# Attention gate's weights split ahead of the third pair's rows, and two steps between a late weight's maximum and its use

## The chip, the cores and the metric

The kernel runs on one core of one Trainium2 chip. The metric is the device time of one execution in microseconds (us). A core has TensorE (PE in the profile, with its weight loads as PEld), VectorE (DVE), ScalarE (ACT), GpSimd (POOL) and SyncE (SP), which issues most of the DMAs. Each engine works through its own list of instructions in order and waits on semaphores for the others.

## The reference, cut to what matters

A one-layer encoder block is applied to two batches of 2048 tokens by 1024 features. Cut to its core:

```python
u = _rmsnorm(h, g_norm)
z = u @ w_in                      # 1024 x 2304
q, k, v, ga, f, gf = jnp.split(z, cuts, axis=-1)   # 512, 128, 128, 512, 512, 512
q = rope(_rmsnorm(q, g_q)); k = rope(_rmsnorm(k, g_k))
a = _blocked_gqa(q, k, v) * jax.nn.silu(ga)        # 8 heads, 2 kv heads, width 64
fo = _fourier_branch(f, w_fmix) * jax.nn.silu(gf)
h = h + jnp.concatenate([a, fo], axis=-1) @ w_out
gate = jax.nn.sigmoid(_rmsnorm(h, g_ple) @ w_ple_gate)
h = h + (p @ w_ple) * gate
y = _rmsnorm(h, g_final)
```

All inputs are float32.

## The kernel before, in words

A float32 product is made of three float16 products. Each operand is split into a high and a low half: ScalarE writes the high half (a scaled copy), VectorE the low half (scaled value minus high half), and TensorE multiplies high by high, high by low and low by high. For a weight the scale is a power of two from the maximum of the whole matrix. So a weight is handled in three stages: eight loads of 128 rows each; eight `tensor_reduce` of VectorE to w_mx (L312), their maximum per partition (L320) and a maximum over partitions by GpSimd (`partition_all_reduce`, p_mm, L322); then VectorE's few instructions on one column that make the scale (`pow2_all`, L269 to L280, whose first writes p_p at L272), and eight splits, each one instruction of ScalarE (L334) and one of VectorE (L335).

The kernel has two phases. In the projection phase, which fills something over a quarter of the span, `project` (L560) handles the tokens in chunks of two tiles of 128 rows ("pairs"). For a chunk it loads the rows x, squares them on ScalarE (`sq_u`), makes the row norm by Newton steps on VectorE (`newton`, result rsq_z at L258), splits the normed rows (`hi_u` on ScalarE at L634, `lo_u` on VectorE at L643, tile hl), and lets SP issue DMA transposes from hl to uc (L438). TensorE then multiplies uc with the q and kv weights (`mm_tile`), and a "sweep" (`sweep_chunk`, L897) multiplies it with f, gf and ga (the attention gate). A sweep gives ScalarE a scaled copy ft or a tanh th (L921, L954) and a copy ge (L913), and VectorE a gt or gat (L956) with its maximum tmax (L944). GpSimd issues the stores of gt, ge and gat. Behind it come the attention and the rest, into which the late parts are filled.

PSUM has eight banks, which `bank` (L169) hands out in a fixed rotation: five ps_x, one ps_f and two ps_g. A bank can be written again only after its readers are done.

The order of instructions on all engines is written out by hand: `manual_schedule` keeps every engine's instructions in the order in which the Python code emits them. Python generators make the order: `next(g)` lets a generator emit its next step, and `until(g, "split")` runs it until it has emitted the last split of a weight.

Ahead of the loop over chunks, L831 to L895 of `project` write the start by hand. The generators there are wkv and wq (kv and q weights) and bg, which goes through f, gf, ga and then the six late weights (`weight_far`, L341: w_out, w_ple_gate and w_ple, each in two halves of 512 columns), the rows p and the channel map. Before the change the lines from L875 run: split gf; a part of the first sweep; square, norm and split the rows of the third pair (number 2: `sq_u(2)`, `newton`, `hi_u(2)`, `lo_u` with its two transposes), three loads of x, and then the whole handling of ga up to its last split (L883), the first w_out loads, a further part of the sweep, and the tables of `mid()`.

A late weight is loaded twice, once for its maximum and once for the split, whose result is stored to DRAM. `weight_far` emits a load per step, the `tensor_reduce` of each (L357), then `scale` (L362): the maximum per partition (L368), the maximum over partitions (in `pow2`, L266), and the scale, all in one step. Three steps later come the splits (L384, L387). In the projection phase a step of bg is taken once in five steps of the sweep (`NBF`, in `sweep_part`), and `defer` emits at once, so a step's place among the sweep's instructions is fixed by that count.

On GpSimd a row named ISA stands ahead of each `partition_all_reduce` of a late weight, and another ahead of the tensor operations that follow it.

Of the kernel before, what the change touches and what calls it, by code (L numbers as in the profile page):

```python
# [10 lines left out]
F32 = mybir.dt.float32  # L11
# [13 lines left out]
W_EXP = 14  # L25
# [115 lines left out]
class Build:  # L141
# [199 lines left out]
    def weight_far(self, name, src, cols, g, pool):  # L341

        nc, st = self.nc, self.st
        sl, ahead, nk = {}, AH, src.shape[0] // 128

        def load(j):
            if j < 2 * nk:
                sl[j] = pool.tile([128, 512], F32, name="w_st", tag="w2k", bufs=self.nw2k)
                nc.sync.dma_start(sl[j][:, :cols], src[j % nk * 128:(j % nk + 1) * 128, :])

        for j in range(ahead):
            load(j)
            yield
        mx = st.tile([128, 8], F32, name="w_mx")
        for k in range(nk):
            load(k + ahead)
            self.defer(lambda w=sl.pop(k), k=k: nc.vector.tensor_reduce(  # L357
                out=mx[:, k:k + 1], in_=w[:, :cols], op=ALU.max, axis=AX.X, apply_absolute_value=True))
            yield
        f = [None] * nk  # L360

        def scale():  # L362
            m = mx
            if g is not None:
                m = st.tile([128, 8], F32, name="w_m2")
                nc.vector.tensor_tensor(out=m[:], in0=mx[:], in1=g[:], op=ALU.mult)
            m1 = st.tile([128, 1], F32, name="w_m1")
            nc.vector.tensor_reduce(out=m1[:], in_=m[:, :nk], op=ALU.max, axis=AX.X, apply_absolute_value=True)  # L368
            s, self.sc[name] = self.pow2("w_" + name, m1[:], W_EXP)
            f[:] = [s[:]] * nk  # L370
            if g is not None:
                gs = st.tile([128, 8], F32, name="w_gs")
                nc.vector.tensor_scalar(out=gs[:], in0=g[:], scalar1=s[:], scalar2=None, op0=ALU.mult)
                f[:] = [gs[:, k:k + 1] for k in range(nk)]

        self.defer(scale)
        self.wd[name] = nc.dram_tensor("wd_" + name, (128, 2, nk, cols), F16, kind="Internal").ap()
        for _ in range(3):
            yield
        for k in range(nk):  # L380
            load(k + nk + ahead)
            w = sl.pop(k + nk)
            o = pool.tile([128, 2, 512], F16, name="w_o", tag="w2k", bufs=self.nw2k)
            nc.scalar.activation(o[:, 0, :cols], w[:, :cols], AF.Copy, scale=f[k])  # L384

            def low(k=k, w=w, o=o):
                nc.vector.scalar_tensor_tensor(out=o[:, 1, :cols], in0=w[:, :cols], scalar=f[k], in1=o[:, 0, :cols],  # L387
                                               op0=ALU.mult, op1=ALU.subtract)
                nc.sync.dma_start(self.wd[name][:, :, k, :], o[:, :, :cols])

            self.defer(low)
            yield
# [167 lines left out]
    def project(self, P, PU, W, early, wkv, wq, wga, bg, mid):  # L560
# [3 lines left out]
        nc, st = self.nc, self.st  # L564
# [27 lines left out]
        def sq_u(i):  # L592
            SU[i] = st.tile([128, CH], F32, name="n_su", bufs=3)
            for tt in range(CH):
                j = P.tile([128, 2 * DM], F16, name="jk", tag="sq", bufs=1)
                nc.scalar.activation(j[:, :DM], X[i][tt][:], AF.Square, accum_out=SU[i][:, tt:tt + 1])
# [6 lines left out]
        def newton(iq, iu, sq):  # L603
            ms = P.tile([128, 11 * CH], F32, name="n_ms", bufs=2)
            q, u = ms[:, :10 * CH].rearrange("p (t h) -> p t h", t=CH), ms[:, 10 * CH:]
            if sq is not None:
                ss = P.tile([128, CH, 10], F32, name="q_ss", bufs=2)
                nc.vector.tensor_reduce(out=ss[:], in_=sq[:], op=ALU.add, axis=AX.X)
                for m, sl, _, _ in heads:
                    nc.vector.tensor_scalar(out=q[:, :, sl], in0=ss[:, :, sl], scalar1=self.sc["ms_" + m][:],  # L610
                                            scalar2=EPS, op0=ALU.mult, op1=ALU.add)
            else:
                nc.vector.memset(ms[:, :10 * CH], 1.0)
            if iu is not None:
                nc.vector.tensor_scalar(out=u, in0=SU.pop(iu)[:], scalar1=1.0 / DM / U_SC ** 2,
                                        scalar2=EPS / U_SC ** 2, op0=ALU.mult, op1=ALU.add)
            else:
                nc.vector.memset(u, 1.0)
            r = self.rsqrt(ms[:], 11 * CH, "q", st=P)
            if iu is not None:  # L620
                R[iu] = r[:, 10 * CH:]
            if sq is not None:
                rq = r[:, :10 * CH].rearrange("p (t h) -> p t h", t=CH)
                rs = P.tile([128, CH, 10], F32, name="q_rs", bufs=2)
                for m, sl, _, _ in heads:
                    nc.vector.tensor_scalar(out=rs[:, :, sl], in0=rq[:, :, sl], scalar1=self.sc["inv_" + m][:],
                                            scalar2=None, op0=ALU.mult)
                return rs

        def hi_u(i):  # L630
            HL[i] = []
            for tt in range(CH):
                hl = PU.tile([128, 2, DM], F16, name="hl", bufs=2)
                nc.scalar.activation(hl[:, 0, :], X[i][tt][:], AF.Copy, scale=R[i][:, tt:tt + 1])  # L634
                HL[i].append(hl)
# [110 lines left out]
        def sweep_part(us):  # L746

            while us > 0 and sweeps:
                try:
                    us -= next(sweeps[0])  # L750
                    if done:
                        done.append(True)
                        if len(done) % NBF == 0:
                            next(bg, None)
                        if len(done) % NBF == 2:
                            next(self.ahead, None)
                except StopIteration:
                    del sweeps[0]
# [16 lines left out]
        def until(g, word):  # L775
            while next(g) != word:
                pass
# [97 lines left out]
        until(bg, "split")  # L875
        sweep_part(10.4)
        sq_u(2)
        newton(None, 2, None)
        hi_u(2)
        both(lo_u, 2)  # L880
        load_x(3, 1)
        both(load_x, 4)
        until(bg, "split")  # L883
        next(bg)
        done.append(True)
        sweep_part(11.6)
        mid()
# [967 lines left out]
```

## Time and profile before

| what | value |
|---|---|
| median of 3 runs | 2743.02 us (2740.77 to 2745.37) |
| profiled execution | 2747.83 us |
| its span | 2746.0 us |
| granted TensorE clock, mean | 0.991 |
| busy: PE, DVE, ACT, POOL | 96%, 62%, 44%, 59% |
| TensorE's wait for the ga split | 7.34 us, ended at 91.20 us |
| TensorE's next long wait | 6.15 us, ended at 144.13 us |
| VectorE's waits for the maximum over partitions of the six late weights | 39.1 us in 6 waits |

A row of the timeline gives the start (us from the span's start), how long the merged instructions took, the engine, the line, the operation with its tiles and the count; the brackets at its end say how long the engine was idle ahead of it and which instruction ended that. SPq is SyncE's queue of issued DMAs. A row of the waits gives who waited for whom: total, times, longest. A row of the DMA view gives the median time from issue to landing.

### The profile page before, as it was taken

Reading aid. Unit: us, or ns where it says so; the run is one execution under the profiler, and the core shown is the slowest. Engines: PE = TensorE matmul, PEld = TensorE weight load, DVE = VectorE, ACT = ScalarE, POOL = GpSimd, SP = SyncE. Lnnn points to the kernel's source line nnn. Section 1 sums busy time; section 2 is a strip of 40 time slices with the busy share of each in tenths; the row PEclk is TensorE's granted clock in tenths of the full one; section 3 lists DMA queues with packets and bytes.
Section 4 is the critical chain, followed back from the end, with each engine's and each line's share of the span. In section 5 each row is a group of like instructions: output and inputs, shape, how many; then the busy total and the mean of one; then the engine's idle time right before and its main releaser. Section 6 shows DMA issues by size and latency. Waiting matters only on the chain.

```text
span 2746.0 us, 46196 instructions
## 1 busy us (share of the span) xinstructions
PE 2649.2 (96%) x18176; PEld 1261.7 (46%) x18176; DVE 1702.8 (62%) x2477; ACT 1213.0 (44%) x2047; POOL 1631.3 (59%) x1394
## 2 busy tenths in 40 slices
PE   6899999999998998999999999999999999999998
PEld 3455565655555553444434444344444334444443
DVE  6755555564455775666666666666666667666644
ACT  3434333342224553454544555445545445444442
POOL 1223323242335886777777777777777777777760
PEclk9999999999999999999999999999999999999999
DMA  7567567675427662122222223322222222222223
GB/s 233 144 177 199 163 192 189 180 189 118 140 71 229 215 215 83 45 60 63 74 61 60 55 67 81 88 63 69 56 79 58 64 70 68 58 72 74 58 68 76
DMA packets 418554, 296.73 MB, mean 108 GB/s; under 512 B 259456, under 2 KB 360000, under 8 KB 418336
## 3 DMA queue, kind: packets, MB, share of 16 engines
q1 hardware_dynamic: 405424, 252.01, 35.0%
q0 software_dynamic: 12912, 41.77, 4.2%
q8 instruction: 142, 2.33, 0.4%
q14 instruction: 76, 0.62, 0.1%
HBM read 149.50 MB, written 86.51 MB: 86 GB/s over the span
## 4 chain that ended last, share of the span: by engine, by line
PE 86%; DVE 6%; issue 2%; DMA 2%; ACT 1%; POOL 1%; SPq 0%; DVEq 0%; ACTq 0%; POOLq 0%
PE ps_g L1473 22%; PE ps_o L1205 16%; PE ps_x L445 15%; PE ps_s L1141 13%; PE ps_f L445 6%; PE ps_g L445 6%; PE ps_m L1168 4%; PE ps_f L1237 1%; DVE a_mx L1176 1%; PE ps_f L1191 1%; PE ps_g L1012 1%; PE ps_g L1060 1%; DVE w_mx L312 1%; ACT p L1144 0%; PE ps_x L911 0%
## 5 line engine op out<-in xcount | busy, mean ns | idle before, releaser
L1149 POOL TENSOR_TENSOR acc<-acc,p 128x1024 f32<-128x1024 f32 x384 | 910.7, 2372 | 217.8 <-ACT p L1144 172.7
L1176 DVE TENSOR_REDUCE a_mx<-ps_m 128x1 f32<-128x1024 f32 x499 | 610.1, 1223 | 529.9 <-PE ps_m L1168 520.8
L1144 ACT ACTIVATE p<-ps_s,s_scale 128x512 f32<-128x512 f32 x1024 | 647.2, 683 | 659.1 <-PE ps_s L1141 645.6
L1473 PE MATMUL ps_g<-w_pg,hT 64*128 64x512 f16 x2784 | 494.8, 377 | 5.8 <-DMA hT<-h_hl 5.7
L1205 PE MATMUL ps_o<-p,v 128*64 128x512 f32 x2048 | 466.1, 597 | 0.0
L445 PEld LDWEIGHTS <-uc 128*128 128x128 f16 x3072 | 301.3, 98 | 311.8 <-issue 22.4
L1141 PE MATMUL ps_s<-q,k 64*128 64x512 f16 x3072 | 435.0, 378 | 4.9 <-ACT p L1144 4.8
L1473 PEld LDWEIGHTS <-hT 64*128 64x128 f16 x2784 | 200.2, 94 | 165.3 <-issue 20.7
L1141 PEld LDWEIGHTS <-k 64*128 64x128 f16 x3072 | 149.6, 94 | 250.8 <-issue 128.0
L1473 PE MATMUL ps_g<-w_wo,mh 64*128 64x512 f16 x1440 | 261.6, 378 | 1.4 <-DVE seen L1439 1.4
L1205 PEld LDWEIGHTS ps_o<-p,v 128*64 128x64 f32 x2048 | 141.7, 137 | 257.3 <-issue 248.2
L1473 PE MATMUL ps_g<-w_wo,mT 64*128 64x512 f16 x1440 | 256.7, 377 | 0.6 <-DMA mT<-mh 0.6
L1168 PE MATMUL ps_m<-k,q 64*128 64x512 f16 x998 | 202.3, 377 | 11.4 <-DVE a_mx L1176 9.6
L1147 POOL TENSOR_TENSOR acc<-p,p 128x1024 f32<-128x1024 f32 x64 | 150.7, 2354 | 97.7 <-ACT p L1144 97.0
L445 PEld LDWEIGHTS <-w_ga 128*128 128x128 f16 x1536 | 151.4, 99 | 53.7 <-issue 23.3
L928 POOL DMA_DIRECT2D gfd<-gt x32 | 19.2, 601 | 216.0 <-DVE gt L956 211.1
L1473 PEld LDWEIGHTS <-mh 64*128 64x128 f16 x1440 | 99.3, 94 | 89.6 <-issue 14.5
L1473 PEld LDWEIGHTS <-mT 64*128 64x128 f16 x1440 | 100.6, 94 | 84.6 <-issue 2.3
L1221 ACT ACTIVATE tb<-ps_o,a_scale 64x256 f32<-64x256 f32 x128 | 60.0, 469 | 167.4 <-PE ps_o L1205 166.6
L445 PE MATMUL ps_x<-uc,w_ga 128*128 128x256 f16 x1008 | 115.8, 276 | 6.8 <-ACT ge L913 6.2
L1244 DVE RECIPROCAL ps_f<-ps_f 128x256 f32<-128x256 f32 x61 | 107.1, 1756 | 14.2 <-PE ps_f L1237 14.2
L946 POOL DMA_DIRECT2D agd<-gat x64 | 35.8, 559 | 134.7 <-DVE gat L956 134.5
(331 smaller groups left out, 3404.2 us busy)
## 6 DMA issues: line engine op xcount, KB each, us to landing
q<-qTd SPq DMA_DIRECT2D x256, 64.0 KB, 2.2
ag<-agd SPq DMA_DIRECT2D x64, 256.0 KB, 3.3
out<-h POOLq DMA_DIRECT2D x31, 512.0 KB, 3.0
x<-in_x_prompt SPq DMA_DIRECT2D x16, 512.0 KB, 5.6
w_st<-in_w_out SPq DMA_DIRECT2D x32, 256.0 KB, 4.3
gfd<-gt POOLq DMA_DIRECT2D x32, 256.0 KB, 3.2
gd<-ge POOLq DMA_DIRECT2D x32, 256.0 KB, 3.6
agd<-gat POOLq DMA_DIRECT2D x64, 128.0 KB, 2.4
```

The costliest lines, as they stand in the source:

```text
L445: self.nc.tensor.matmul(ps, lhs(ia, k), rhs(ib, k), start=(i == 0), stop=(i == 3 * ks - 1))
L946: nc.gpsimd.dma_start(self.agd[s][1, r * 128:(r + 1) * 128, c * n:(c + 1) * n], gt[:, :n])
L1141: nc.tensor.matmul(S[u][e][:], w[sl], q[sl].rearrange("p h q -> p (h q)"), start=j == i == 0, stop=i + 1 == len(todo), skip_group_check=True)
L1144: nc.scalar.activation(p[:, e, :], S[u][e][:], AF.Exp, scale=self.sc["s_scale"][:])
L1147: nc.gpsimd.tensor_tensor(out=ACC[u][:], in0=P[u, 0][:], in1=p[:], op=ALU.add)
L1149: nc.gpsimd.tensor_tensor(out=ACC[u][:], in0=ACC[u][:], in1=p[:], op=ALU.add)
L1168: nc.tensor.matmul(ps[c], Q[u][0][sl, h, :], kt[s, kv, half][sl, :, 0, :], start=True, stop=True)
L1176: nc.vector.reduce_max(MX[u][:, h, half, c:c + 1], x, axis=AX.X)
L1205: nc.tensor.matmul(o[64 * e:64 * e + 64, :], vt[s, kv, c // 8][:, c % 8, :], p[:, e, :], start=(j == 0), stop=(j == 7))
L1221: nc.scalar.activation(tb[64 * e:64 * e + 64], ov[64 - 64 * e:128 - 64 * e, e], AF.Copy, scale=self.sc["a_scale"][64 - 64 * e:128 - 64 * e ...
L1244: nc.vector.reciprocal(r, r)
L1473: nc.tensor.matmul(g[0][:], g[1](ia, k)[sl], g[2](ib, k)[sl], start=a, stop=z, skip_group_check=True)
```

## The change

In `project` the ga weight's eight maxima and its maximum over partitions (nine steps of bg) are emitted right behind `sq_u(2)`, and its scale and its eight splits right behind the third pair's norm. The split of the third pair's rows (`hi_u(2)`, `lo_u`, the transposes) and the three loads of x follow. Before, ga came behind all of these. The first w_out loads come behind the x loads, before and after.

In `weight_far` the maximum over partitions stays in `scale`, but the instructions that use it (`pow2_all` and the column scales) are a function of their own, `factors`, which is emitted two steps later; the splits follow one step behind it, three behind `scale` as before.

```diff
@@ weight_far
         f = [None] * nk
+        mm = st.tile([128, 1], F32, name="p2_mm")
 
         def scale():
...
             nc.vector.tensor_reduce(out=m1[:], in_=m[:, :nk], op=ALU.max, axis=AX.X, apply_absolute_value=True)
-            s, self.sc[name] = self.pow2("w_" + name, m1[:], W_EXP)
+            nc.gpsimd.partition_all_reduce(mm[:], m1[:], 128, bass_isa.ReduceOp.max)
+
+        def factors():
+            s, self.sc[name] = self.pow2_all("w_" + name, mm, W_EXP)
             f[:] = [s[:]] * nk
...
         self.defer(scale)
...
-        for _ in range(3):
+        for _ in range(2):
             yield
+        self.defer(factors)
+        yield
@@ project
         sq_u(2)
+        for _ in range(9):
+            next(bg)
         newton(None, 2, None)
+        until(bg, "split")
+        next(bg)
         hi_u(2)
         both(lo_u, 2)
         load_x(3, 1)
         both(load_x, 4)
-        until(bg, "split")
-        next(bg)
         done.append(True)
```

On TensorE and on SP the order of instructions is the same before and after the change; on GpSimd too, but for buffer numbers. On ScalarE the two high halves of the third pair move behind the eight splits of ga. VectorE's order changes there and at five of the six late weights. The lines of the changed kernel are 1 to 8 higher than the same lines before.

## The prediction

> **What bounds the kernel now.** I read the page first (busy times, chain), then what TensorE waited for, then the timelines of all queues from 70 to 300 us, where the change lies.
>
> ```profile
> span 2746.0 us, 46196 instructions
> PE 2649.2 (96%) x18176; PEld 1261.7 (46%) x18176; DVE 1702.8 (62%) x2477; ACT 1213.0 (44%) x2047; POOL 1631.3 (59%) x1394
> PE 86%; DVE 6%; issue 2%; DMA 2%; ACT 1%; POOL 1%; SPq 0%; DVEq 0%; ACTq 0%; POOLq 0%
> ```
>
> TensorE (PE) is busy 96% of the span and is 86% of the chain that ended last. Nothing behind the projection rests on a clock time, so what TensorE's stream loses or wins early is carried to the end. What counts is therefore TensorE's waits up to 300 us, by what it waited for (total, times, longest):
>
> ```profile
> PE ps_f L445 <- ACT w_ga L334: 7.3, 1, 7.3
> PE ps_x L445 <- ACT ge L913: 6.2, 1, 6.2
> PE ps_g L445 <- DVE gat L956: 5.5, 3, 3.4
> ```
>
> The first is the wait for the attention gate's split (w_ga), the second ends at 144 us, the longest of the third at 296 us. TensorE's timeline at these places and between them:
>
> ```profile
> 91.20 0.61 PE L445 MATMUL ps_f<-uc,w_ga 128*128 128x256 f16 x2 [7.34 <-ACT w_ga L334]
> 104.60 5.34 PE L445 MATMUL ps_x<-wr_q,uc 128*128 128x512 f16 x24
> 122.76 5.34 PE L445 MATMUL ps_f<-w_gf,uc 128*128 128x512 f16 x24
> 128.19 1.12 PE L911 MATMUL ps_x<-ft,dft 128*128 128x512 f32 x2
> 144.13 5.28 PE L445 MATMUL ps_x<-uc,w_ga 128*128 128x256 f16 x24 [6.15 <-ACT ge L913]
> 295.79 4.45 PE L445 MATMUL ps_g<-uc,w_ga 128*128 128x256 f16 x24 [3.44 <-DVE gat L956]
> ```
>
> **Part 1: the gate's split goes ahead of the third pair's rows.** On VectorE (DVE), between the end of the gf weights' split and the gate's scale, before the change (rsq_z is the third pair's row norm, hl its low half, w_mx the gate's maxima, p_p the first step of its scale):
>
> ```order
> L258 TENSOR_TENSOR rsq_z_738<-rsq_z_733,rsq_w 128x22
> L643 SCALAR_TENSOR_TENSOR hl<-x,rsq_z_738,hl 128x1024 x2
> L312 TENSOR_REDUCE w_mx<-w_qn 128x1 x2
> L312 TENSOR_REDUCE w_mx<-w_t_418 128x1 x2
> L312 TENSOR_REDUCE w_mx<-w_t_589 128x1 x2
> L312 TENSOR_REDUCE w_mx<-w_t_592 128x1 x2
> L317 TENSOR_TENSOR w_m_768<-w_mx,gn 128x8
> L320 TENSOR_REDUCE w_m_770<-w_m_768 128x1
> L272 TENSOR_SCALAR p_p<-p_mm 128x1
> ```
>
> and where hl stands now, behind the last of the gate's splits:
>
> ```order
> L335 SCALAR_TENSOR_TENSOR w_ga<-w_t_592,w_gs,w_ga 128x512 x2
> L284 TENSOR_SCALAR inv_ga<-w_ga_i 128x1
> L284 TENSOR_SCALAR h_ga<-inv_ga 128x1
> L649 SCALAR_TENSOR_TENSOR hl<-x,rsq_z_753,hl 128x1024 x2
> L964 SCALAR_TENSOR_TENSOR gt<-th,ps_x 128x512
> L357 TENSOR_REDUCE w_mx<-w_st 128x1
> L964 SCALAR_TENSOR_TENSOR gt<-th,ps_g 128x512
> ```
>
> The maxima now start right behind h_gf, the norm fills the wait for POOL, and the two hl stand just ahead of the first L357. That one reduces the first rows of w_out, so it waits for their load. On SyncE's queue (SP) nothing is reordered; this piece is the same in both:
>
> ```order
> L438 DMA_TRANSPOSE uc<-hl 128x16x128 x2
> L589 DMA x<-in_x_prompt 128x1024 x3
> L349 DMA w_st<-in_w_out 128x512 x3
> ```
>
> So the transposes of hl, which now come late, hold back three x loads and the w_out loads. The rows for the sum:
>
> ```profile
> 75.48 0.15 DVE L284 TENSOR_SCALAR h_gf<-inv_gf 128x1 f32<-128x1 f32 x1
> 77.65 0.17 DVE L615 TENSOR_SCALAR n_ms<-n_su 128x2 f32<-128x2 f32 x1 [1.99 <-ACT jk L596]
> 81.42 2.48 DVE L643 SCALAR_TENSOR_TENSOR hl<-x,rsq_z,hl 128x1024 f16<-128x1024 f32 x2 [1.22 <-ACT hl L634]
> 83.81 1.27 DVE L312 TENSOR_REDUCE w_mx<-w_qn 128x1 f32<-128x512 f32 x2
> 88.88 0.16 DVE L320 TENSOR_REDUCE w_m<-w_m 128x1 f32<-128x8 f32 x1
> 89.59 0.15 DVE L272 TENSOR_SCALAR p_p<-p_mm 128x1 f32<-128x1 f32 x1 [0.55 <-POOL p_mm L322]
> 96.67 0.15 DVE L284 TENSOR_SCALAR h_ga<-inv_ga 128x1 f32<-128x1 f32 x1
> 97.33 0.68 DVE L357 TENSOR_REDUCE w_mx<-w_st 128x1 f32<-128x512 f32 x1
> 80.23 2.19 ACT L634 ACTIVATE hl<-x,rsq_z 128x1024 f16<-128x1024 f32 x2 [2.61 <-DVE rsq_z L258]
> 90.42 1.33 ACT L334 ACTIVATE w_ga<-w_qn,w_gs 128x512 f16<-128x512 f32 x2 [8.01 <-DVE w_gs L328]
> 82.73 4.52 SPq L438 DMA_TRANSPOSE uc<-hl  x2
> 87.31 1.81 SPq L589 DMA_DIRECT2D x<-in_x_prompt  x3
> 89.16 1.84 SPq L349 DMA_DIRECT2D w_st<-in_w_out  x3
> uc<-hl SPq DMA_TRANSPOSE x1, 4.4
> w_st<-in_w_out SPq DMA_DIRECT2D x1, 256.0 KB, 6.1
> ```
>
> The last two rows are landing times from the queue view: the first transpose, issued at 82.73, and the first w_out load, issued at 89.16.
>
> Step by step, in us of the span. After h_gf (75.63) come maxima and their maximum, 83.9 to 89.04, 5.15; the norm, 77.65 to 80.23, 2.6 with its memset; then scale and start of the split, 89.59 to 90.42, 0.8. ScalarE's first split starts at 75.63 + 5.15 + 2.6 + 0.8 = 84.2 in place of 90.42, and TensorE takes it up at 85.0 in place of 91.20: **6.2 earlier**. POOL's 0.55 is hidden by the norm; without that cover it would cost 0.55 again.
>
> The eight splits keep their pace, so h_ga ends at 96.82 - 6.2 = 90.6. There hl starts, 9.2 later than 81.42 (its high half is ready: ScalarE's splits end 6.2 earlier too, near 89.1, and one high half takes 1.1). The transposes, the x loads and the first w_out load leave SP 9.2 later: 89.16 + 9.2 = 98.4, landing 6.1 later at 104.5. VectorE is at L357 by 90.6 + 2.5 (hl) + 0.6 (gt) = 93.7, waits 10.8, and reduces at 104.5 in place of 97.33: **7.2 later**. The transposes themselves are no loss: the first is issued at 91.9 and lands 4.4 later at 96.3, ahead of TensorE, which needs it at 104.60 - 6.2 = 98.4. On ScalarE the two high halves (2.19) now stand ahead of gf's th and ge, which come 4 earlier all the same; POOL's order is unchanged. Queued behind VectorE's wait are the second gt, the g_q and g_k tables, the next row norm and the gat of the first chunk.
>
> Does TensorE feel it? It arrives 6.2 early, until it needs what VectorE and ScalarE give back:
>
> ```profile
> 116.63 0.41 DVE L956 SCALAR_TENSOR_TENSOR gat<-th,ps_f 128x256 f32<-128x256 f32 x1
> 124.71 0.69 DVE L357 TENSOR_REDUCE w_mx<-w_st 128x1 f32<-128x512 f32 x1 [7.22 <-DMA w_st<-in_w_out]
> 127.45 1.26 ACT L921 ACTIVATE ft<-ps_g,inv_f 128x512 f32<-128x512 f32 x2
> ```
>
> Bank ps_f, written at 91.20, is written next at 122.76, after the gat at 116.63 has read it. TensorE would now come at 116.6, the gat ends at 117.0 + 7.2 = 124.2: a wait of 7.6. Then the first L911 needs ft, 127.45 + 7.2; before, TensorE used it 0.7 after its start, so there was no slack, and L911 starts 7.2 late. VectorE's 7.22 wait at 124.71 moves along, since its load stands behind the next transposes on SP, which follow VectorE's next hl. The 6.15 wait at 144.13 ends behind the same chain. So TensorE passes 144.13 at 151.3: part 1 costs **+7.2**. Bounds: the load's landing. x loads and stores beside it could stretch it by one store, 3.6; 0 is the nearest case (the loads at 119 to 121 had stores beside them and landed in 6.0). The lower bound is the load landing in time, -3.6 (rival 1). I take 0.
>
> ```profile
> w_st<-in_w_out SPq DMA_DIRECT2D x3, 256.0 KB, 6.0
> gfd<-gt POOLq DMA_DIRECT2D x1, 256.0 KB, 3.6
> ```
>
> A rule against this reading: the Trainium skill, Perfetto Trace Analysis, section Optimization Strategy, says to find the gaps of the engine one optimizes for and to make what they wait for start sooner. By it, part 1 is worth -6.2, the gap that shrinks; the trace agrees that the gap is there (7.34) but has VectorE's wait at its other end.
>
> **Part 2: two steps between the maximum over partitions and its use.** It concerns the six late weights (w_out, w_ple_gate, w_ple, two halves each). The waits at the second and third:
>
> ```profile
> 203.89 0.15 DVE L272 TENSOR_SCALAR p_p<-p_mm 128x1 f32<-128x1 f32 x1 [6.88 <-POOL p_mm L266]
> 204.59 0.41 DVE L956 SCALAR_TENSOR_TENSOR gat<-th,ps_x 128x256 f32<-128x256 f32 x1
> 205.38 0.41 DVE L956 SCALAR_TENSOR_TENSOR gat<-th,ps_x 128x256 f32<-128x256 f32 x1
> 256.43 0.15 DVE L272 TENSOR_SCALAR p_p<-p_mm 128x1 f32<-128x1 f32 x1 [6.93 <-POOL p_mm L266]
> ```
>
> On VectorE at the second weight, now:
>
> ```order
> L369 TENSOR_REDUCE w_m_1945<-w_m_1943 128x1
> L964 SCALAR_TENSOR_TENSOR gat<-th,ps_x 128x256
> L952 TENSOR_REDUCE tmax_87<-gat 128x1
> L272 TENSOR_SCALAR p_p<-p_mm 128x1
> L273 TENSOR_SCALAR p_p<-p_p 128x1
> ```
>
> One gat and its tmax, which stood behind the wait, now stand inside it. At the first weight no row of VectorE lies between, so its wait (part of the chain to 144.13) stays. VectorE still waits for POOL, but has one pair, 205.38 - 204.59 = 0.79, less to do behind it. The chain of waits runs from these two places to 295.79, so the 3.44 there shrinks by up to 2 x 0.79: **-1.6**. Bounds: 0, if another releaser comes last, and -3.4, if that wait goes. At the fourth weight the scale now stands behind the next row norm; TensorE did not wait there, and the splits' stores followed that norm before too: nothing.
>
> **Sum.** +7.2 - 1.6 = +5.6. The profiled execution took 2747.83 (span 2746.0 and 1.8 around it), so 2753.4; it lies 4.8 above the median of the three runs, 2743.02, so the forecast there is **2748.6**, +0.20%. About 0.2%, 5.5 us, is what a measurement can tell from no change; the forecast lies right on that edge.
>
> **Rivals.**
> 1. *Faster: the w_out load does not hold VectorE.* Place: L357 on VectorE. Then VectorE is at 93.7 in place of 97.33, 3.6 ahead, and TensorE's second wait ends 3.6 earlier: -3.6 - 1.6 = -5.2, 2737.8. It decides at a landing before 97.33 + 1.6 = 98.9; 104.5 speaks against it, and so does SP's unchanged order. For it: nothing on SP but position holds the load. It is where the Trainium skill's rule on gaps leads. 0.14.
> 2. *No change that can be measured: +7.2, but the 3.44 wait goes entirely*: +3.8, 2746.8. For it: several steps of that chain are VectorE's, and each may win a little. Against: only 1.6 is found in the order. 0.18.
> 3. *More: the moved loads meet stores, landing 3.6 later, and part 2 gives nothing*: +10.8, 2753.8. Against: loads with stores beside them landed in 6.0. 0.08.
>
> That part 2 does not do what it says holds for the first weight, and is in the sum.
>
> **How the numbers follow.** The forecast's case has 0.60: +4 to +7.5, about 0.42 of it above 5.5 and 0.18 below. Slower 0.42 + 0.08 = 0.50; within 0.2% 0.18 + 0.18 = 0.36; faster 0.14. The range leaves out most of rival 1 and keeps rival 3: 2740.5 to 2754.
>
> **What would show it.** Right: the w_ga wait of TensorE falls from 7.3 to near 1.3; VectorE waits about 11 at the first L357 for w_st; TensorE has a new wait of some 7 at ps_f for gat and passes the stretch of 144.13 about 7 later; the wait at 295.79 (then near 303) is about 1.9. Wrong: L357 without a wait, or w_ga passed early and 144.13 passed before 144. Then rival 1 holds.

## The result, and the profile after

| kernel | median | range |
|---|---|---|
| before, 6 runs beside it | 2745.01 us | 2740.77 to 2747.75 |
| after, 6 runs | 2754.85 us | 2751.39 to 2755.97 |

The change makes the kernel slower: ratio 1.0035, 95% interval 1.0025 to 1.0046, so +9.6 us (6.9 to 12.6). The forecast was +5.6, and its range, up to 2754, ended just below the median. Before's own median was 2743.02 in the three runs that the forecast started from and 2745.01 here, so of the 6.3 us between 2748.6 and 2754.85 2.0 are the starting point and 4.3 the change. Of all executions here and in the experiments three ran far slower (3084, 4593 and 10609 us), and the ratios leave them out.

The profiled execution of after took 2751.89, near the fast end of its range, and that of before 2747.83, above its median. The pair shown here therefore differs by 4.1 us only; a second profiled execution of after, further down, took 2757.74.

The page of after, in the rows that answer to those of before:

```profile
span 2750.1 us, 46195 instructions
PE 2648.5 (96%) x18176; PEld 1260.3 (46%) x18176; DVE 1699.7 (62%) x2477; ACT 1212.9 (44%) x2047; POOL 1631.6 (59%) x1394
```

TensorE does the same work. Its waits between 80 and 320 us that come to over 0.5 us (total, times, longest):

```profile
PE ps_f L451 <- DVE gat L964: 7.4, 1, 7.4
PE ps_x L919 <- ACT ft L929: 4.6, 1, 4.6
PE ps_x L451 <- ACT ge L921: 2.9, 1, 2.9
PE ps_g L451 <- DVE gat L964: 2.9, 1, 2.9
PE ps_f L451 <- DVE w_ga L335: 1.4, 7, 0.4
PE ps_f L451 <- ACT w_ga L334: 0.9, 1, 0.9
```

The gate's wait is gone, 0.9 in place of 7.3, with seven short ones for single splits behind it (1.4 in all, in place of 0.3). Two stand here that before did not have, 7.4 at bank ps_f and 4.6 at ft. TensorE's timeline:

```profile
85.72 0.39 PE L451 MATMUL ps_f<-uc,w_ga 128*128 128x256 f16 x2 [0.91 <-ACT w_ga L334]
124.89 7.91 PE L451 MATMUL ps_f<-w_gf,uc 128*128 128x512 f16 x24 [7.44 <-DVE gat L964]
137.40 2.08 PE L919 MATMUL ps_x<-ft,dft 128*128 128x512 f32 x2 [4.59 <-ACT ft L929]
151.56 2.78 PE L451 MATMUL ps_x<-uc,w_ga 128*128 128x256 f16 x24 [2.92 <-ACT ge L921]
300.17 4.45 PE L451 MATMUL ps_g<-uc,w_ga 128*128 128x256 f16 x24 [2.90 <-DVE gat L964]
```

In this profile TensorE began its 48 matmuls of w_f, which lie ahead of everything that the change moves, at 62.22 and not at 61.27 as in before; so 0.95 comes off every later start when the two are compared. TensorE is then 6.4 early at 85.72 (forecast 6.2) and 6.5 late at 151.56, where before it passed at 144.13. VectorE, ScalarE, SP and POOL between:

```profile
91.26 2.47 DVE L649 SCALAR_TENSOR_TENSOR hl<-x,rsq_z,hl 128x1024 f16<-128x1024 f32 x2
107.30 0.69 DVE L357 TENSOR_REDUCE w_mx<-w_st 128x1 f32<-128x512 f32 x1 [12.97 <-DMA w_st<-in_w_out]
118.51 4.81 DVE L649 SCALAR_TENSOR_TENSOR hl<-x,rsq_z,hl 128x1024 f16<-128x1024 f32 x2 [0.31 <-ACT hl L640]
132.09 0.69 DVE L357 TENSOR_REDUCE w_mx<-w_st 128x1 f32<-128x512 f32 x1 [6.79 <-DMA w_st<-in_w_out]
...
103.91 1.06 ACT L602 ACTIVATE jk<-x 128x1024 f16<-128x1024 f32 x1 [8.73 <-DMA x<-in_x_prompt]
...
92.56 7.06 SPq L444 DMA_TRANSPOSE uc<-hl  x2
99.68 1.51 SPq L595 DMA_DIRECT2D x<-in_x_prompt  x3
101.24 1.90 SPq L349 DMA_DIRECT2D w_st<-in_w_out  x3
...
94.63 0.74 POOL L936 DMA_DIRECT2D gfd<-gt  x1 [12.38 <-DVE gt L964]
118.93 3.31 POOL L691 TENSOR_TENSOR qn<-z,q_rs 128x1280 f32<-128x1280 f32 x1
```

VectorE waits 13.0 us for w_out's first rows, where the forecast had a wait of 10.8, and reduces them 9.0 later than before (107.30 - 0.95 - 97.33). Two things were not forecast. The two transposes hold SP for 7.06 us in place of 4.52; two of POOL's four stores of the first sweep, which before came ten us after the transposes, now leave in the midst of them. And ScalarE waits 8.7 us too, for an x load that stands behind the same transposes. The first of these stores in the kernel before:

```profile
97.72 0.74 POOL L928 DMA_DIRECT2D gfd<-gt  x1 [8.16 <-DVE gt L956]
```

### The profile page after: what moved, and what is told of

Read it like the earlier page. It is cut to its first block, busy times and chain, and to the rows that moved or that the text cites. A ratio compares the mean times of both kernels' runs of the same rounds, so it can differ in the third digit from the quotient of the medians.

```text
span 2750.1 us, 46195 instructions
## 1 busy us (share of the span) xinstructions
PE 2648.5 (96%) x18176; PEld 1260.3 (46%) x18176; DVE 1699.7 (62%) x2477; ACT 1212.9 (44%) x2047; POOL 1631.6 (59%) x1394
## 4 chain that ended last, share of the span: by engine, by line
PE 86%; DVE 7%; DMA 3%; issue 2%; ACT 1%; POOL 1%; SPq 1%; DVEq 0%; ACTq 0%; POOLq 0%
PE ps_g L1481 22%; PE ps_o L1213 16%; PE ps_x L451 15%; PE ps_s L1149 13%; PE ps_f L451 6%; PE ps_g L451 6%; PE ps_m L1176 4%; PE ps_f L1245 1%; DVE a_mx L1184 1%; PE ps_f L1199 1%; PE ps_g L1020 1%; PE ps_g L1068 1%; DVE w_mx L312 1%; ACT p L1152 0%; PE ps_x L919 0%
```

## The experiments

The theories that the expectations speak of: *A*, the first w_out load stands behind the late transposes, VectorE waits for it, and that is the loss. *B*, part 2 costs what the forecast did not see. *C*, the third pair's rows come too late themselves, and the load is a bystander. *D*, formed after the fourth run: two transfers stand behind the transposes, and either alone holds the chain. All ratios are to the kernel before in the same job (medians 2745.8 to 2746.8 us). Lines in the experiments' kernels stand up to 14 higher; L358 and L364 are the change's L357 in the rows of w_mx.

**1. Part 1 alone.** The edit in `project` only; `weight_far` as before.

> Part 1 alone: the gate's split ahead of the third pair's rows, the late weights as before the change. Theory A (the first w_out load stands behind the late transposes on SP, VectorE waits for it, and every long wait of TensorE is followed by slow matmuls): part 1 carries the whole loss, +9 to +11 us against the kernel before, about the change's 9.7 plus the 0.5 that part 2 won at the 3.44 wait. Theory B (the loss above the forecast comes from part 2): part 1 gives the forecast's +7.2 or less, and the rest is missing here. Theory C (the third pair's rows themselves come too late, not the load): the same as A here.

Ratio 1.0034 (1.0022 to 1.0046), 2755.16 us: +9.3. Part 1 carries the whole loss, and B is out.

**2. Part 2 alone.** The edit in `weight_far` only.

> Part 2 alone: the two steps between a late weight's maximum over partitions and its use, the start as before the change. Theory A: between -1.6 and 0 us, most likely -0.5, what the traces show at the wait near 296. Theory B: slower by 2 to 5 us, from instructions that the scale now stands behind at the later weights. Theory C says nothing on it.

Ratio 1.0000 (0.9991 to 1.0009), 2745.41 us. The waits for the maximum over partitions do get shorter, 25.1 us in all in place of 39.1, and TensorE's wait behind them hardly does:

```profile
DVE p_p L272 <- POOL p_mm L370: 25.1, 5, 6.8
```

and in TensorE's timeline:

```profile
296.06 4.43 PE L451 MATMUL ps_g<-uc,w_ga 128*128 128x256 f16 x24 [2.75 <-DVE gat L962]
```

2.75 in place of 3.44: 0.7 us, and the matmuls behind it are as slow as before (4.43 for 24). The interval, 2.5 us to either side, can't tell -0.7 from the forecast's -1.6; the row can.

**3. The change with w_out's first two loads ahead of the third pair's transposes.** No other engine's order changes.

```diff
@@ weight_far
+        pre = 2 if name == "wo0" else 0
+        for j in range(pre):
+            load(j)
+        if pre:
+            yield
         for j in range(ahead):
-            load(j)
+            if j >= pre:
+                load(j)
             yield
...
-            load(k + ahead)
+            if k + ahead >= pre:
+                load(k + ahead)
@@ project
         until(bg, "split")
         next(bg)
+        next(bg)
         hi_u(2)
```

> The changed kernel with w_out's first two loads issued on SP ahead of the third pair's transposes; nothing else changes its place. Theory A: the first L357 has no wait, VectorE is there near 94.4 in place of 107.3, three ahead of before; the wait at the fourth L357 stays, since its load is still behind the next transposes, but ends some 3 earlier than in the kernel before; total -3 to -5 us against before, -12 to -14 against the change. Theory C: the first L357's wait goes, but TensorE still waits at ps_f or ft for VectorE or ScalarE work behind the late rows, and the total stays 3 us or more above before.

Ratio 1.0016 (1.0007 to 1.0024), 2750.28 us: +4.4, half the loss, not the gain that A asked for. The first L357 has no wait now (93.31). VectorE, then ScalarE, then TensorE:

```profile
107.39 1.49 DVE L621 TENSOR_REDUCE q_ss<-sq 128x20 f32<-128x1280 f32 x1 [8.36 <-ACT sq L613]
...
104.91 1.06 ACT L609 ACTIVATE jk<-x 128x1024 f16<-128x1024 f32 x1 [10.67 <-DMA x<-in_x_prompt]
...
148.15 5.08 PE L458 MATMUL ps_x<-uc,w_ga 128*128 128x256 f16 x24 [4.57 <-ACT ge L929]
```

VectorE waits 8.4 us a little further on, for ScalarE's square sq; sq stands in ScalarE's queue behind the square of x, which waits 10.7 for the load of the fourth pair's second row tile. That load is the first of the three x loads, behind the transposes as well. It was hidden under VectorE's own wait. So A names one of two holders; D takes its place.

**4. The same with six w_out loads early.** `pre = 6` in the edit of 3.

> The same with w_out's first six loads ahead of the third pair's transposes, so that the wait of VectorE at the fourth L357 (6.8 us, ending at 132) can go too. Theory A: TensorE's wait of 6.15 at 144 (2.92 in the changed kernel) goes for the most part; -7 to -11 us against before. It would be less if the six buffers, which are out of the ring of ten for so long, hold up the sweep's copies (ft, th, ge), which would show as new waits of ScalarE. Theory C: no better than with two loads, and above before.

Ratio 1.0008 (0.9999 to 1.0016), 2747.73 us: +2.2. ScalarE still waits 9.05 for x at 106.25. Six loads do help at the next place, but the seventh is behind the next transposes and waits in turn:

```profile
130.24 0.69 DVE L364 TENSOR_REDUCE w_mx<-w_st 128x1 f32<-128x512 f32 x1 [4.67 <-DMA w_st<-in_w_out]
```

**5. The x load and two w_out loads early.** As 3, and in `project`:

```diff
         next(bg)
+        load_x(3, 1)
         next(bg)
         hi_u(2)
         both(lo_u, 2)
-        load_x(3, 1)
         both(load_x, 4)
```

> The changed kernel with the load of the fourth pair's second row tile and w_out's first two loads ahead of the third pair's transposes on SP. Theory D (two transfers stood behind the transposes, not one: the first w_out load, which holds VectorE, and that x load, which holds ScalarE's square, 8.7 us at L602 in the changed kernel and 10.7 with the two w_out loads early; either alone is enough to hold the chain): VectorE's wait for sq (8.4 with the two loads) goes, its next hl stands at 104 to 105 in place of 113, TensorE has no wait at ps_f and little at ft; what is left is the wait at the fourth L357; -3 to -6 us against the kernel before. Theory C (the late rows of the third pair as such): still 3 us or more above before.

Ratio 0.9980 (0.9971 to 0.9989), 2740.76 us: -5.5, faster than before. VectorE's next hl stands at 105 in place of 118.5, and TensorE has no wait left at ps_f and 0.8 at ft. What is left is the wait at the fourth L357 (7.15) and TensorE's behind it:

```profile
92.39 7.25 SPq L451 DMA_TRANSPOSE uc<-hl  x2
...
105.25 4.55 DVE L656 SCALAR_TENSOR_TENSOR hl<-x,rsq_z,hl 128x1024 f16<-128x1024 f32 x2 [0.44 <-ACT hl L647]
...
123.25 1.12 PE L927 MATMUL ps_x<-ft,dft 128*128 128x512 f32 x2 [0.80 <-ACT ft L937]
138.41 5.28 PE L458 MATMUL ps_x<-uc,w_ga 128*128 128x256 f16 x24 [5.38 <-ACT ge L929]
```

The transposes of the third pair are as late here as in the change, and hold SP as long. So C is out.

**6. Two of the three x loads and six w_out loads early.** As 5, with `pre = 6` and:

```diff
         next(bg)
+        load_x(4, 0)
         hi_u(2)
         both(lo_u, 2)
-        both(load_x, 4)
+        load_x(4, 1)
```

> As the last one, with one more x load and six w_out loads ahead of the transposes. Theory D: the wait at the fourth L357 goes too or falls to a few us; -6 to -11 us against before. Against it: loads 7 and 8 of w_out stay behind the next transposes and may wait as they did with six loads alone (4.7 us).

Ratio 0.9969 (0.9957 to 0.9980), 2737.55 us: -8.5, the fastest here. The wait that was left has moved to the seventh L357:

```profile
120.31 1.28 DVE L364 TENSOR_REDUCE w_mx<-w_st 128x1 f32<-128x512 f32 x2 [5.04 <-DMA w_st<-in_w_out]
...
136.60 4.45 PE L458 MATMUL ps_x<-uc,w_ga 128*128 128x256 f16 x24 [3.60 <-ACT ge L930]
```

**7. The control: the kernel before with the loads of 6.** `load_early` issues the first loads of the late weight, and `weight_far` takes them over.

```diff
         newton(None, 2, None)
+        load_x(3, 1)
+        self.load_early("wo0", self.a["w_out"][0][:, :512], 6, P)
+        load_x(4, 0)
         hi_u(2)
         both(lo_u, 2)
-        load_x(3, 1)
-        both(load_x, 4)
+        load_x(4, 1)
```

> The kernel before the change with the same x and w_out loads ahead of the third pair's transposes, as a control: how much of the gain is the loads' own. The 7.2 us wait at the fourth L357 goes or shrinks, and with it part of TensorE's 6.15 at 144. Theory D: -3 to -6 us against before, and some 3 to 6 more than the same loads with the change, since the gate's wait of 7.3 us at 91 stays. If it is as fast as the changed kernel with the same loads, splitting the gate earlier is worth nothing even when no transfer is held.

Ratio 0.9973 (0.9963 to 0.9982), 2739.43 us: -7.4. Nearly all of 6 is the loads' own gain. With the gate split late TensorE still waits 7.34 there, and then hardly any more at ge:

```profile
92.12 0.61 PE L453 MATMUL ps_f<-uc,w_ga 128*128 128x256 f16 x2 [7.34 <-ACT w_ga L335]
139.72 2.78 PE L453 MATMUL ps_x<-uc,w_ga 128*128 128x256 f16 x24 [0.39 <-ACT ge L923]
```

In 6 it comes to the gate 6.7 earlier (85.42; 6.4 when both are counted from the w_f matmuls, 61.91 there and 62.19 here) and waits 3.6 at ge, with 1.7 of slow matmuls behind it (4.45 in place of 2.78): behind these it is 1.2 ahead. The medians differ by 1.9 us, and the intervals overlap, so the two runs alone do not tell this from nothing. The difference holds part 2 as well, which 6 has and 7 has not.

**8. The first sweep's four stores off the transposes.** In the changed kernel the stores of gfd and gd are issued on SP behind the first w_out loads, not on POOL.

```diff
+        put = self.late.append if (s, c) == (0, 0) else lambda f: f()
...
-            nc.gpsimd.dma_start(self.gd[s][:, t, :], ge[:])
+            put(lambda: (nc.sync if (s, c) == (0, 0) else nc.gpsimd).dma_start(self.gd[s][:, t, :], ge[:]))
...
         sweep_part(11.6)
+        for f in self.late:
+            f()
         mid()
```

> The changed kernel with the four stores of the first sweep (gfd, gd), which POOL issues beside the third pair's transposes, issued on SP behind the first w_out loads. Theory S (the transposes hold SP for 7.06 in place of 4.52 us because these stores are under way): the hold falls to 4.5 to 5, x and w_out loads leave 2 to 2.5 earlier, the wait at the first L357 shrinks by as much; -1.5 to -3 us against the change, so +6.5 to +8 against before. Rival (the hold has another cause, or varies from run to run): no change, +9 to +10.

Ratio 1.0029 (1.0019 to 1.0039), 2753.86 us: +8.0. The transposes' hold falls as S said; the first w_out load then takes 7.1 us from issue to L357 in place of 6.0:

```profile
92.22 4.98 SPq L445 DMA_TRANSPOSE uc<-hl  x2
99.16 1.89 SPq L350 DMA_DIRECT2D w_st<-in_w_out  x3
...
106.30 0.69 DVE L358 TENSOR_REDUCE w_mx<-w_st 128x1 f32<-128x512 f32 x1 [12.32 <-DMA w_st<-in_w_out]
```

So the stores cause the longer hold, and moving them behind the loads gives half of it back, presumably because they now share the loads' time. The total moved by less than the measurement can tell.

**9. The x load alone early.** The changed kernel with nothing but:

```diff
         next(bg)
+        load_x(3, 1)
         hi_u(2)
         both(lo_u, 2)
-        load_x(3, 1)
```

> The changed kernel with only the load of the fourth pair's second row tile ahead of the third pair's transposes; w_out's loads stay behind them. It fills the fourth place of a table of two by two (none early 9.6 above before; two w_out loads early 4.5 above; x and two w_out loads 5.8 below). Theory D (two transfers, either of which holds the chain alone): the first L357 still waits some 12 us for w_st, ScalarE's square no longer waits, VectorE waits little or not for sq behind L357; nearly the whole loss stays, +8 to +10 against before. Rival (each transfer has its own share that adds): about 10 less than with the w_out loads alone, so near or below before.

Ratio 1.0030 (1.0018 to 1.0041), 2755.00 us: +8.2. The first L357 waits 11.57, and no wait for sq follows. The table of two by two, as us against before (ratio less one, by 2746):

| | w_out behind | two w_out loads ahead |
|---|---|---|
| x load behind | +9.6 | +4.4 |
| x load ahead | +8.2 | -5.5 |

The x load alone gives 1.4, the w_out loads alone 5.2, both 15.1. Shares that add would give 6.6. That is D's pattern: either is enough to hold most of the chain.

**10. The change with everything early.** As 6, with w_out's seventh and eighth load behind the last x load, ahead of the next transposes.

```diff
@@ weight_far
         if pre:
             yield
+            load(6)
+            load(7)
+            pre = 8
+            yield
@@ project
         load_x(4, 1)
+        next(bg)
         done.append(True)
```

> The changed kernel with both x loads and six w_out loads ahead of the third pair's transposes, and the seventh and eighth right behind the last x load, ahead of the next transposes, so that the wait of 5.0 at the seventh L357 can go. Theory D: TensorE's wait of 3.6 at 136.6 and the slow matmuls behind it (4.45 in place of 2.78) go; -11 to -14 against before. Against it: eight buffers of the ring of ten are then held, and the sweep's gat or th may wait for one.

Ratio 0.9981 (0.9973 to 0.9990), 2741.11 us: -5.2, by the medians 3.6 behind 6, though the intervals still overlap. No L357 waits any more, but the ring of ten buffers is now what is short: VectorE, ScalarE and TensorE wait for the stores that free one.

```profile
98.13 0.69 DVE L978 SCALAR_TENSOR_TENSOR gt<-th,ps_g 128x512 f32<-128x512 f32 x1 [3.45 <-DMA gfd<-gt]
...
124.58 0.47 ACT L976 ACTIVATE th<-ps_x,h_ga 128x256 f32<-128x256 f32 x1 [11.52 <-DMA agd<-gat]
...
130.02 2.07 PE L933 MATMUL ps_x<-ft,dft 128*128 128x512 f32 x2 [7.63 <-ACT ft L943]
```

**11. The kernel before with the same.** The edit of 7, and `load_early` once more, up to 8, behind `load_x(4, 1)`.

> The kernel before the change with the same loads early. TensorE hardly waited at 139.7 any more with six (0.39 us), so the two more should bring little: -7 to -8.5 against before. The difference to the changed kernel with the same loads then is what the earlier split of the gate is worth when no transfer is held: by theory D 4 to 6 us; by the rival that the 6.2 us won at the gate's split come back at another wait in any case, under 2.

Ratio 0.9989 (0.9981 to 0.9998), 2743.04 us: -3.0, by the same shortage (a gt waits 3.52 for a store). By the medians the change is 1.9 us ahead, as between 6 and 7, and here too the intervals overlap. So with the loads early the change as a whole, part 2 with it, is worth about 2 if anything. The 4 to 6 that D expected did not come; the rows of 6 and 7 bear out the rival in the expectation, that most of the lead comes back at another wait.

**12. The change once more.**

> The changed kernel once more, timed in more rounds beside the others, for the size of the loss: +9 to +11 against before if the median of the first result holds; +4 to +6 if the two profiled executions, 4.1 us apart, are the better measure.

Ratio 1.0035 (1.0021 to 1.0049), 2756.82 us: +9.6 again. Its profiled execution took 2757.74, and shows where the other one was lucky. Of this kernel VectorE, TensorE, SP and POOL:

```profile
107.55 0.69 DVE L357 TENSOR_REDUCE w_mx<-w_st 128x1 f32<-128x512 f32 x1 [12.91 <-DMA w_st<-in_w_out]
119.30 6.48 DVE L649 SCALAR_TENSOR_TENSOR hl<-x,rsq_z,hl 128x1024 f16<-128x1024 f32 x2 [0.29 <-ACT hl L640]
135.53 0.69 DVE L357 TENSOR_REDUCE w_mx<-w_st 128x1 f32<-128x512 f32 x1 [7.78 <-DMA w_st<-in_w_out]
...
62.52 10.52 PE L451 MATMUL ps_x<-w_f,uc 128*128 128x512 f16 x48
127.34 7.13 PE L451 MATMUL ps_f<-w_gf,uc 128*128 128x512 f16 x24 [9.58 <-DVE gat L964]
155.04 4.36 PE L451 MATMUL ps_x<-uc,w_ga 128*128 128x256 f16 x24 [3.47 <-ACT ge L921]
306.50 5.28 PE L451 MATMUL ps_g<-uc,w_ga 128*128 128x256 f16 x24 [4.17 <-DVE gat L964]
...
92.87 7.04 SPq L444 DMA_TRANSPOSE uc<-hl  x2
101.52 1.79 SPq L349 DMA_DIRECT2D w_st<-in_w_out  x3
...
119.08 2.33 POOL L691 TENSOR_TENSOR qn<-z,q_rs 128x1280 f32<-128x1280 f32 x1 [0.24 <-DVE q_rs L632]
```

The two hl of the fourth pair took 6.48 us here (6.49 in before, 4.81 in the first profile of after): here POOL's qn (the normed q and k, an operation of GpSimd on whole tiles) began 0.2 us ahead of them, there 0.4 behind. TensorE's wait at ps_f was 9.58, not 7.44. The matmuls behind the 3.47 took 4.36, where those behind the 2.92 took 2.78.

## Why the prediction was right or wrong

**Part 1's mechanism was right.** The gate's split starts earlier, TensorE takes it up at 84.8 (85.72 - 0.95; forecast 85.0), VectorE is held at the first L357, TensorE pays at ps_f, and is late from there on. Experiment 1 puts the whole loss in this part, 3 against 9 shows the two w_out loads as the larger holder.

**The step that was mis-sized: the queue on SP.** The prediction moved the transposes, the x loads and the first w_out load by 9.2 and kept their durations: "landing 6.1 later at 104.5". In the second profile of after, whose start is 1.25 later than before's (62.52; the same stretch began at 61.27 in before), the load leaves SP at 101.52 - 1.25 = 100.3, not 98.4. The transposes began on time (92.87 - 1.25 = 91.6, forecast 91.9); they held SP for 7.04 in place of 4.52. So L357 is 107.55 - 1.25 - 97.33 = 9.0 late, not 7.2. The prediction had looked for stores beside the *loads* and bounded that at 3.6 in rival 3; they stood beside the transposes ahead of them. The loads at 119 to 121 that it leaned on had one store of half the size beside them (agd at 117.33), and the transposes before them none. Of the profiles with the late transposes and POOL's stores beside them eight show a hold of 7.0 to 7.9 and one (experiment 3) 5.65, with 4.23 for the three x loads behind it in place of 1.5 to 1.8; those without these stores beside them show 4.4 to 5.0 (before and experiments 2, 7, 8 and 11).

In the kernel before, TensorE's start of the stretch, the two hl of the fourth pair and the store at 117.33:

```profile
61.27 10.52 PE L445 MATMUL ps_x<-w_f,uc 128*128 128x512 f16 x48
...
109.02 6.49 DVE L643 SCALAR_TENSOR_TENSOR hl<-x,rsq_z,hl 128x1024 f16<-128x1024 f32 x2 [0.29 <-ACT hl L634]
...
117.33 0.74 POOL L946 DMA_DIRECT2D agd<-gat  x1 [1.23 <-DVE gat L956]
```

From there the loss is carried, as forecast, but not unchanged. The fourth L357 adds 0.6 (135.53 - 1.25 - 124.71 = 9.6; its wait is 7.78 in place of 7.22). TensorE passes 144.13 at 155.04 - 1.25 = 153.8, 9.7 late (forecast 7.2), and with 0.9 less of slow matmuls behind it (4.36 in place of 5.28) 8.8. Behind the wait at 306 it is 10.3 late. The two spans differ by 10.0, less 1.25 again 8.8, inside the measured 6.9 to 12.6. The first profile of after gives 4.0 where this one gives 8.8: VectorE came to hl 0.5 sooner and was through with them 1.7 sooner (4.81 against 6.48), waited 1.0 less at the fourth L357 (6.79 against 7.78), and TensorE had no slow matmuls behind ge (1.6).

**Part 2, "up to 2 x 0.79: -1.6", was too large.** The pair gat and tmax did move into the wait, but TensorE's wait at 296 shrank by 0.7 (experiment 2 against before) and by 0.3 (4.17 with both parts in experiment 12, 4.44 with part 1 alone in experiment 1). It bounded this at 0, and 0 is what the total shows. That VectorE's waits for POOL fell by 14 us says nothing by itself: all but 0.3 to 0.7 of it was time that VectorE had to spare. The first late weight's wait did not move (3.60 against 3.54), as forecast. The row of 5.5 us in three waits that the prediction lists is of the whole span: of the three only the 3.44, which the sum uses, lies ahead of 300 us; the others are at 493 and 742.

**A holder was overlooked, and it would have changed rival 1.** The prediction followed the three x loads onto SP's queue and named the 9.2, but not who reads them. Had the w_out load not held VectorE, rival 1's "-5.2" would not have come: experiment 3 is that case, and it was +4.4, since the x load holds ScalarE's square and with it VectorE. Both together reach the number that rival 1 gave (-5.5), but not by its terms, so the match is luck: rival 1 had 3.6 from VectorE's lead and 1.6 from part 2. In experiment 5 the wait that part 2 was to shorten is 3.79, no shorter than the 3.44 of before, and 1.9 of VectorE's lead is the shorter hl (4.55 against 6.49). No run has these three loads early in the kernel before, so what is the loads' own share of it stays open.

**The rule on gaps.** The Trainium skill, Perfetto Trace Analysis, section Optimization Strategy (find the engine's gaps and start earlier what they wait for), was weighed at -6.2 for the gate's gap. The runs do not agree: the gap went (7.34 to 0.91), and with its cost removed by hand (6 against 7, 10 against 11) the medians gained 1.9, which the intervals do not tell from nothing, where 6.2 was to come. The gate's 7.3 us were for the most part slack for what comes at 120 to 145, where VectorE, ScalarE and the loads set the pace; a TensorE that comes earlier waits there: in experiment 6 it is 6.4 ahead of 7 at the gate and 1.2 ahead behind ge.

## What to carry to other kernels

When a step moves later in the program, list everything that is queued behind its DMAs and who reads each of those transfers; removing the first holder that the trace names may only uncover the second, which was hidden under it. Durations do not move with a row: ask what will be in flight beside it at the new place, and before filling a gap of the bounding engine ask whether the next thing that it needs would also come earlier. Loads that need nothing but a buffer belong ahead of an issue that waits for a computation: that alone was worth 7 us here, as long as the ring of buffers could bear it.

## What the runs showed of the hardware

- **Slow matmuls behind a wait.** 24 matmuls of 128x256 take 2.78 us, and took that behind waits of 0.39, 1.03, 1.72 and once 2.92 us. Behind the other waits between 130 and 320 us, 2.46 to 6.25 long, they took 4.28 to 5.28, and not more behind the longer ones: 4.45 behind 2.46 (experiment 8), 5.28 behind 4.17, 4.46 behind 6.14 (experiment 9), 4.36 behind 6.25 (experiment 2). So a wait costs up to 2.5 more than its length, unless the next wait hides it. It is the granted clock, the last column but two of after's windows, which follow the 7.44 us wait:

```profile
124.00:126.00 2.00, 1.11 (x3) 0.41 (x3) 1.26 (x3) 0.47 (x1) 2.00 (x2) 0.50 0.80 154
128.00:130.00 2.00, 2.00 (x7) 0.64 (x5) 0.00 (x0) 0.00 (x0) 0.00 (x0) 0.50 0.95 385
130.00:132.00 2.00, 2.00 (x11) 0.91 (x10) 0.00 (x0) 0.04 (x1) 0.00 (x0) 0.97 1.02 390
```

It stands at 0.50 for some five us behind the wait and is back at 0.97 by 130 to 132. In the clock records of all these profiles the stretches at half speed between 80 and 320 us last 3.41, 6.83 or 10.24 us, so one, two or three times 3.41. That fits a cost that does not grow with the wait. The Trainium skill, TensorE: Matmul & The Clock Gate, section HAM oscillation — how this bites in real kernels, says that an idle gap longer than about 3.4 us makes the clock fall back. The rows from 3.44 up agree; but behind 2.46, 2.75, 2.90, 3.29 and 3.37 the same 24 took 4.35 to 4.45, so here it began below that.
- **VectorE beside GpSimd.** The two hl take 2.47 to 2.48 us at the third pair, where POOL stands idle. At the fourth pair they took 5.96 to 6.50 us where POOL's qn had begun 0.2 to 0.7 ahead of them, and 4.55 to 4.81 where it began 0.15 to 0.4 behind. In experiments 7 and 10 they came ahead of qn and took 2.96 and 2.48; there POOL's rt (the rotary tables), an operation beside them, took 1.73 and 1.23 in place of 0.7. So which of the two begins first, by a few tenths, goes with 1.7 of the 4.8 us between the two profiles of the changed kernel (6.48 against 4.81). The Trainium skill, GPSIMD Engine Reference, section 1. Specifications, says that GpSimd's interface to SBUF is shared with VectorE and that instructions with two SBUF inputs contend for it; hl has two inputs, and the trace agrees. No kernel here separated the two, so it is read from the rows only.
- **Transposes and stores.** The third pair's two DMA transposes held SP's queue for 4.4 to 5.0 us without GpSimd's stores beside them and, but for one case of 5.65, for 7.0 to 7.9 with them; experiment 8, which moves the stores alone, took it from 7.0 to 5.0.
